# Rope queries of the latent heads made pair by pair, a second query buffer for every second head, and their zeros on GpSimd

## The chip, the cores and the metric

The kernel runs on one core of a Trainium2 chip. The metric is the device time of one execution in microseconds (us). Before the change three runs took 2487.42, 2492.72 and 2490.44 us: the median is 2490.44 us.

## The reference, cut to what matters

A trunk of two layers works on 256 latent tokens and 256 context tokens of width 2048, batch 1. The first layer runs two kinds of attention heads side by side and projects their gated outputs back to the stream; the second is a gated DeltaNet layer. The change lies in the first layer, in its eight latent-attention heads (MLA). The queries, keys and values of such a head come from low-rank latents; a query has 128 plain dimensions (`qn`) and 64 rotated ones (`qr`), and the rotated key part `kr` is common to all heads:

```
q = to_heads(rmsnorm(cq) @ w_qb, 8)            # 192 = 128 plain + 64 rope, per head
kv = to_heads(rmsnorm(ckv) @ w_kvb, 8)         # 256 = 128 key + 128 value
s_lat = (qn @ kn.T + rope(qr) @ rope(kr).T) * 192 ** -0.5      # latent keys
s_ctx = (qn @ kn_c.T + rope(qr) @ kr_c.T) * 192 ** -0.5        # context keys
p = softmax over both;  o = p_lat @ v + p_ctx @ v_c
```

The context tokens get the same attention over context keys alone. All inputs and outputs are float32.

## The kernel before, in words

**Tiling.** Activations lie with features on the 128 partitions and the 512 tokens (256 latent, 256 context) along the free axis. A matrix product with a weight tile of 128 by 128 is `dense`: each float32 factor is split in a rounded part and a remainder (`hi` and `lo`, or the two halves of `hx`, `cx`, `gx`), and three matmuls (lines L90, L91, L92) add hi·hi, hi·lo and lo·hi into a PSUM tile `mm`, of which there are two. A weight is loaded on the SyncE queue (`raw`, four buffers, L71), ScalarE casts it to `whi` (L77) and VectorE makes `wlo` (L78); both have three buffers.

**The stage around the change.** The layer runs seven neighbourhood heads, then makes the latents `craw` (eight tiles of 128 by 512), then loads the eighth neighbourhood head's inputs (`na7`). Now `cx`, which takes the place of `hx` in SBUF, receives in its first half `ch` the latents' hi parts (ScalarE, L468) and lo parts (VectorE, L469, `cx<-craw,cx`), and in its second half `qr` the rope queries. When `craw` has been read, its place is given to a pool with three buffers `mraw`, for the modulation weights of the second layer, and one of the size `lacc`. `attend` of the eighth neighbourhood head follows, then the rope queries of all eight latent heads, in four pairs: a `dense` of 12 matmuls from one weight of 2048 columns, zeros for the other head's 64 partitions (ScalarE, L481), and `roped`, which scales (L449), multiplies by a permutation on TensorE (`pp`, L451), combines with sine and cosine (L453 to L455), and writes hi and lo parts into `qr`. Then each of the eight heads makes `qT`, `kT` and `vT` (12 matmuls each) and runs `attend`: scores `sp` (L365), row maximum `mx` (VectorE, L389), exponential `pr` (ScalarE, L392), sum and scaling (L394, L395), transposes `pt` (L398), hi and lo parts `PT` (L357, L358), the product `po` with the values, and the gate (L405). `qT`, `kT` and `vT` have one buffer each.

**What sets the order.** In this layer the instructions aren't issued in the order of the source: a planner places them on each engine by its own estimate of when operands are ready, source order first among those that are. Each engine then works through its list strictly in that order. Between the heads lie steps of `ahead`, a generator that computes modulation chunks of the second layer: a chunk of 512 columns needs 16 TensorE matmuls into `pmod` (L141) from eight `mraw` loads of 512 KB (L136), then a copy and four transposes `pmt`. Each `mraw` load covers two of the 16 matmuls. Four chunks (2, 3, 8 and 9) fall in this stage. In the trace each float32 matmul (`pmod`, `pp`) shows as two.

After the heads, `gx` takes the place of `cx`: the gated outputs are split again (L502, L503) and the output projection begins; on VectorE four further chunks (L175, L177, `lacc`) run beside it.

Of the kernel before, what the change touches and what calls it, by code (L numbers as in the profile page):

```python
# [10 lines left out]
AF = mybir.ActivationFunctionType  # L11
ALU = mybir.AluOpType
# [6 lines left out]
T = 512  # L19
# [7 lines left out]
def trunk_kernel(ctx: ExitStack, tc: tile.TileContext, g):  # L27
    nc = tc.nc
    V, A, PE, P = nc.vector, nc.scalar, nc.tensor, nc.gpsimd
# [14 lines left out]
    def cst(name, shape, src=None):  # L44
        t = const.tile(shape, F32, name=name, tag=name)
        if src is not None:
            nc.scalar.dma_start(t, src)
        return t
# [3 lines left out]
    ones = cst("ones", [128, 128])  # L52
# [16 lines left out]
    def load_raw(src, n=1024):  # L69
        raw = wp.tile([128, 1024], F32, name="raw", tag="raw", bufs=4)  # L70
        nc.sync.dma_start(raw[:, :n], src)  # L71
        return raw
# [8 lines left out]
    def load_split(src, n=2048):  # L81
        return [split(load_raw(src[:, c:min(n, c + 1024)], min(1024, n - c)), min(1024, n - c))
                for c in range(0, n, 1024)]

    def dense(ps, w, off, kt, xh, xl, k0=0, sl=slice(0, T), first=True, last=True):
        for k in range(kt):
            c = off + k * 128
            wh, wl = w[c // 1024]
            c = slice(c % 1024, c % 1024 + 128)
            PE.matmul(ps, wh[:, c], xh[:, k0 + k, sl], start=first and k == 0, stop=False)  # L90
            PE.matmul(ps, wh[:, c], xl[:, k0 + k, sl], start=False, stop=False)  # L91
            end = PE.matmul(ps, wl[:, c], xh[:, k0 + k, sl], start=False, stop=last and k == kt - 1)  # L92
        return end.ins
# [166 lines left out]
    with tc.tile_pool(name="s0", bufs=2) as tp, tc.tile_pool(name="s0p", bufs=1, space=PSUM) as ps:  # L260
# [37 lines left out]
        for j, (k0, n) in enumerate(GROUPS):  # L298
            ahead = mods_of(j + 1) if j < end else iter(())
            for i in range(0, NS, 2):  # L300
                own = i < NP
                p = [pz[i + e] if own else mm_tile() for e in range(2)]
# [16 lines left out]
    with tc.tile_pool(name="ab", bufs=2, reuse_waits="tile") as tp, \  # L319
            tc.tile_pool(name="abp", bufs=2, space=PSUM, reuse_waits="tile") as ps:  # L320
        u, last_mm = NS, None
        mr = tc.alloc_tile_pool(name="mr", bufs=2)
# [21 lines left out]
        for j in range(NS, KT):  # L344
            p = unit(hh, hl)
# [3 lines left out]
        def parts(src, name, n=T, scale=1.0, pool=None, bufs=1):  # L349

            t = (pool or tp).tile([128, 2, n], F32R, name=name, tag=name, bufs=bufs)
            both(t[:, 0], t[:, 1], src, scale)
            return t
# [53 lines left out]
        def keep(p, name):  # L407
            t = tp.tile([128, T], F32, name=name, tag=name, bufs=1)
            A.copy(t, p)
            return t  # L410
# [33 lines left out]
        def roped(p, scale, parts_of):  # L444
            out = tp.tile([128, T], F32, name="rope", tag="rope", bufs=1)
            if scale == 1.0:
                A.copy(out, p)
            else:
                A.mul(out, p, scale)  # L449
            pp = ps.tile([128, S], F32, name="pp", tag="tr", bufs=TR)  # L450
            PE.matmul(pp, perm, out[:, :S], start=True, stop=True)  # L451
            t = tp.tile([128, S], F32, name="rtmp", tag="mtmp")
            V.tensor_tensor(t, pp, sinT, op=ALU.mult)  # L453
            V.tensor_tensor(out[:, :S], out[:, :S], cosT, op=ALU.mult)
            V.tensor_tensor(out[:, :S], out[:, :S], t, op=ALU.add)  # L455
            for r, hi, lo in parts_of:
                both(hi, lo, out[r])
# [5 lines left out]
        ch, qr = cx[:, 0], cx[:, 1]  # L463
        for i, gain in enumerate((q_gain, kv_gain)):
            for k in range(4):
                j = 4 * i + k
# [4 lines left out]
        mr = tc.alloc_tile_pool(name="mr2", bufs=2, reuse_waits="tile")  # L471
        ahead = later(mr, ((1, (2, 3, 8), 0),))

        rows = slice(0, 64), slice(64, 128)
        attend(*na7)
        w = load_split(g["ab_wqr"])
        for j in range(4):
            p = mm_tile()
            dense(p, w, j * 512, 4, ch, ch[:, 8:])
            for e in range(2):  # L480
                A.activation(qr[rows[1 - e], 4 * j + 2 * e:4 * j + 2 * e + 2],  # L481
                             ones[rows[1 - e], 0:1].unsqueeze(2).broadcast_to([64, 2, T]), AF.Copy, scale=0.0)
            roped(p, MLA_SCALE, [(rows[e], *[qr[rows[e], 4 * j + 2 * e + i] for i in range(2)]) for e in range(2)])
        for h in range(8):
            w = load_split(g["ab_wb"][h], 1536)
            o = []
            for j, (k0, name, sc) in enumerate(((0, "qT", MLA_SCALE), (4, "kT", 1.0), (4, "vT", 1.0))):
                p = mm_tile()
                last_mm = dense(p, w, j * 512, 4, ch, ch[:, 8:], k0)
                o.append(keep(p, name) if name == "vT" else parts(p, name, scale=sc))  # L490
            steps(ahead, 1)
            attend(*o, 8 + h, None, ([qr[:, 2 * h + i] for i in range(2)], [kr[:, i] for i in range(2)]))

# [12 lines left out]
        for j in range(KT):  # L506
# [3 lines left out]
            p = unit(gh, gl, g["ab_wo"][j])  # L510
# [129 lines left out]
    with tc.tile_pool(name="dn", bufs=2, reuse_waits="tile") as tp, \  # L640
# [12 lines left out]
        ch = cons[:, 0:768].rearrange("p (a n) -> p a n", a=6)  # L653
# [3 lines left out]
        p = dunit(U_BA, FULL)  # L657
# [562 lines left out]
        for st in range(-2, 64 + LAG):  # L1220
            i, n = st // 4, st % 4
            j, m = (st - LAG) // 4, (st - LAG) % 4
# [86 lines left out]
        for u in [v for e in range(KT - NE) for v in (e, NE + e)]:  # L1309
            k0 = 24 if u < NE else 0  # L1310
            w = load_split(g["dn_wo"][u][:, 128 * k0:], 4096 - 128 * k0)
            p = mm_tile() if i % 2 else ps.tile([128, T], F32, name="mm2", tag="ks")
            if i < KT - 1:
                dense2(p, w, 0, 32 - k0, gx, k0=k0)
            else:
                p = p[:, :S]
# [123 lines left out]
```

## Time and profile before

| | us |
|---|---|
| median of three runs | 2490.44 |
| profiled execution, its own time | 2493.04 |
| its span, from first to last instruction | 2491.2 |
| TensorE busy in the span | 2428.2 (97%) |
| VectorE busy | 1762.8 (71%) |
| ScalarE busy | 1105.6 (44%) |
| GpSimd busy | 161.1 (6%) |
| the stage, from `na7`'s first scores to the second output tile | about 687.6 to 907 |

The profiled execution is 2.6 us above the median, and 1.8 us of its time lie outside the span. Rows of the timeline give the start and the length in us, the engine, the line, the operation, the tiles written and read, and in brackets the idle time before and what ended it. A row of the chain of waits gives start, length and the piece of work. TensorE rows overlap, as matmuls are pipelined: the pitch from one to the next is what a matmul costs, and the busy time overstates it. The mean granted clock was 0.992.

### The profile page before, as it was taken

The numbers are of one execution on the slowest core, as the hardware profiler recorded it, in microseconds if no ns is written. First come the engines' busy times: TensorE is split into PE (matmuls) and PEld (weight loads), VectorE is DVE, ScalarE is ACT, GpSimd is POOL, SyncE is SP. The second block draws the span as 40 slices with busy tenths as digits, with TensorE's granted clock in tenths as the row PEclk, the third lists the DMA queues.
The fourth block names the chain that finished last, engine by engine and source line by source line (L and its number), as shares of the span: only waits on it lengthen the run. The fifth ranks groups of instructions, "written<-read, shape, count | busy, mean of one in ns | idle before, by whom it ended". The sixth has DMA issues, their size and how long they took to land.

```text
span 2491.2 us, 42483 instructions
## 1 busy us (share of the span) xinstructions
PE 2428.2 (97%) x16110; PEld 1963.1 (79%) x16110; DVE 1762.8 (71%) x3538; ACT 1105.6 (44%) x2446; POOL 161.1 (6%) x165
## 2 busy tenths in 40 slices
PE   6999999999989999999999999999999999999998
PEld 4557888888858878858998989987777777777787
DVE  4654678883356687856998988885777777777765
ACT  4223332333254432257565655634444544445453
POOL 0000000000000000020011101000000000012000
PEclk9999999999999999999999999999999999999999
DMA  8872645542253366664665666774343333336454
GB/s 252 282 277 87 200 154 172 169 157 84 88 187 110 102 198 204 226 210 136 195 173 158 179 178 180 204 201 108 87 116 103 115 112 98 106 100 184 148 193 141
DMA packets 254940, 397.24 MB, mean 159 GB/s; under 512 B 122257, under 2 KB 163857, under 8 KB 254609
## 3 DMA queue, kind: packets, MB, share of 16 engines
q1 hardware_dynamic: 253584, 393.00, 52.0%
q8 instruction: 127, 2.08, 0.3%
q10 hardware_dynamic: 1152, 1.54, 0.2%
q14 instruction: 77, 0.62, 0.1%
HBM read 356.94 MB, written 35.39 MB: 157 GB/s over the span
## 4 chain that ended last, share of the span: by engine, by line
PE 88%; issue 5%; DMA 3%; DVE 2%; ACT 1%; SPq 0%; POOL 0%; DVEq 0%; POOLq 0%; ACTq 0%
PE mm L90 21%; PE mm L91 20%; PE mm L92 20%; PE pks L1033 3%; PE pmod L141 3%; PE ptr L1045 2%; PE sp L365 2%; PE mm L105 2%; PE po L365 1%; DMA mraw<-dn_wm 1%; PE ptr L1078 1%; PE psu L1064 1%; PE pks L1064 1%; PE pt L398 1%; PE mm L107 1%
## 5 line engine op out<-in xcount | busy, mean ns | idle before, releaser
L90 PE MATMUL mm<-hx,whi 128*128 128x512 f32 (+1 forms) x2304 | 843.7, 366 | 2.3 <-ACT t L664 2.2
L91 PE MATMUL mm<-hx,whi 128*128 128x512 f32 (+1 forms) x2304 | 820.6, 356 | 2.5 <-issue 2.5
L92 PE MATMUL mm<-hx,wlo 128*128 128x512 f32 (+1 forms) x2304 | 819.4, 356 | 0.6 <-DVE wlo L78 0.6
L77 ACT CAST whi<-raw 128x1024 fp32r<-128x1024 f32 (+2 forms) x346 | 338.6, 980 | 701.4 <-PE mm L91 502.3
L78 DVE TENSOR_TENSOR wlo<-raw,whi 128x1024 fp32r<-128x1024 f32 (+2 forms) x346 | 394.3, 1142 | 204.3 <-ACT whi L77 198.2
L90 PEld LDWEIGHTS mm<-hx,whi 128*128 128x128 f32 x2304 | 438.8, 190 | 106.3 <-issue 27.0
L92 PEld LDWEIGHTS mm<-hx,wlo 128*128 128x128 f32 x2304 | 438.6, 190 | 65.1 <-issue 4.2
L91 PEld LDWEIGHTS mm<-hx,whi 128*128 128x128 f32 x2304 | 438.8, 190 | 61.4 <-issue 9.2
L177 DVE SCALAR_TENSOR_TENSOR lacc<-mraw,cond,lacc 128x512 f32<-128x512 f32 x300 | 208.6, 746 | 0.7 <-DMA mraw<-dn_wm 0.7
L585 DVE SCALAR_TENSOR_TENSOR acc<-cin,taps,acc 128x508 f32<-128x508 f32 (+3 forms) x256 | 187.2, 731 | 20.3 <-ACT acc L576 17.2
L105 PE MATMUL mm<-hx,whi 128*128 128x512 f32 x480 | 173.1, 404 | 0.1
L1055 DVE SCALAR_TENSOR_TENSOR vl<-ptr,egm,vh 128x128 fp32r<-128x128 f32 x224 | 64.7, 346 | 95.1 <-ACT rf L1052 37.9
L107 PE MATMUL mm<-hx,wlo 128*128 128x256 f32 x457 | 128.4, 281 | 1.3 <-DVE wlo L1139 1.2
L141 PE MATMUL pmod<-mraw,cond 128*32 128x512 f32 (+2 forms) x640 | 98.4, 508 | 28.1 <-DMA mraw<-ab_wm 18.8
L1139 DVE TENSOR_TENSOR wlo<-raw,whi 128x1024 fp32r<-128x1024 f32 x84 | 102.5, 1221 | 13.5 <-ACT whi L1131 13.4
L105 PEld LDWEIGHTS mm<-hx,whi 128*128 128x128 f32 x480 | 88.9, 188 | 24.5 <-issue 5.0
L816 DVE SCALAR_TENSOR_TENSOR outer<-L,bv,X 128x31 f32<-128x31 f32 (+15 forms) x248 | 99.4, 401 | 6.4 <-POOL X L811 0.5
L90 PE MATMUL mm<-gx,whi 128*128 128x512 f32 x256 | 100.3, 394 | 3.4 <-DVE x1B L515 2.4
L599 ACT ACTIVATE ac<-acc 128x128 f32<-128x128 f32 x160 | 37.4, 300 | 144.2 <-DVE acc L585 144.1
L91 PE MATMUL mm<-gx,whi 128*128 128x512 f32 x256 | 100.4, 392 | 0.5 <-DVE gx L503 0.5
L92 PE MATMUL mm<-gx,wlo 128*128 128x512 f32 x256 | 99.8, 391 | 0.0
L1049 ACT ACTIVATE vh<-ptr,egm 128x128 fp32r<-128x128 f32 x224 | 71.3, 374 | 57.1 <-PE ptr L1045 55.2
(301 smaller groups left out, 3648.5 us busy)
## 6 DMA issues: line engine op xcount, KB each, us to landing
raw<-dn_w SPq DMA_DIRECT2D x194, 512.0 KB
mraw<-dn_wm SPq DMA_DIRECT2D x96, 512.0 KB
mraw<-ab_wm SPq DMA_DIRECT2D x88, 512.0 KB
raw<-ab_w SPq DMA_DIRECT2D x66, 512.0 KB
raw<-dn_wo SPq DMA_DIRECT2D x64, 512.0 KB
raw<-ab_wo SPq DMA_DIRECT2D x32, 512.0 KB
raw<-ab_w SPq DMA_DIRECT2D x32, 256.0 KB
spt<-sp SPq DMA_DIRECT2D x64, 128.0 KB
```

The costliest lines, as they stand in the source:

```text
L77: A.copy(hi[:, :m], raw[:, :m])
L78: V.tensor_tensor(lo[:, :m], raw[:, :m], hi[:, :m].bitcast(F32), op=ALU.subtract)
L90: PE.matmul(ps, wh[:, c], xh[:, k0 + k, sl], start=first and k == 0, stop=False)
L91: PE.matmul(ps, wh[:, c], xl[:, k0 + k, sl], start=False, stop=False)
L92: end = PE.matmul(ps, wl[:, c], xh[:, k0 + k, sl], start=False, stop=last and k == kt - 1)
L105: PE.matmul(p2, wh[:, c], x[:, :, k0 + k], start=start, stop=stop)
L107: PE.matmul(p2[:, 0], wl[:, c], x[:, 0, k0 + k], start=False, stop=False)
L141: PE.matmul(pmod[32 * q:32 * q + 32, :m], cond[:, 4 * kg + q, :], raw[c // 1024][:, half + c % 1024:half + c % 1024 + m], start=kg == 0, s ...
L177: V.scalar_tensor_tensor(acc[:, s], raw[:, q], cond[:, k, s:s + 1], acc[:, s], op0=ALU.mult, op1=ALU.add)
L585: V.scalar_tensor_tensor(o3[:, :, i0:i1], p3[:, :, i0 + d:i1 + d], taps[:, ch, t:t + 1], o3[:, :, i0:i1], op0=ALU.mult, op1=ALU.add)
L816: V.scalar_tensor_tensor(o, L[:, rows, k:k + 1].broadcast_to([128, n, m]), bv[:, k:k + 1], X[:, k:k + 1, cols].broadcast_to([128, n, m]), ...
L1139: V.tensor_tensor(w, raws[j], h.bitcast(F32), op=ALU.subtract)
```

## The change

The rope queries of pair j are now made by a function `rope_pair(j)`, which loads only the 512 weight columns of its pair. Pair 0 is made before the first latent head; pairs 1, 2 and 3 are made in the heads 1, 3 and 5, between their `vT` and their `attend`. The plain queries of heads 1, 3, 5 and 7 go into the buffer `lacc` of the `mr2` pool instead of `qT`. The zeros are written by GpSimd as a constant minus itself, where ScalarE multiplied a constant by 0. Line numbers after the change are 7 higher from L498 on.

```diff
         attend(*na7)
-        w = load_split(g["ab_wqr"])
-        for j in range(4):
+
+        def rope_pair(j):
+            w = load_split(g["ab_wqr"][:, 512 * j:512 * j + 512], 512)
             p = mm_tile()
-            dense(p, w, j * 512, 4, ch, ch[:, 8:])
+            dense(p, w, 0, 4, ch, ch[:, 8:])
             for e in range(2):
-                A.activation(qr[rows[1 - e], 4 * j + 2 * e:4 * j + 2 * e + 2],
-                             ones[rows[1 - e], 0:1].unsqueeze(2).broadcast_to([64, 2, T]), AF.Copy, scale=0.0)
+                one = ones[rows[1 - e], 0:1].unsqueeze(2).broadcast_to([64, 2, T])
+                P.tensor_tensor(qr[rows[1 - e], 4 * j + 2 * e:4 * j + 2 * e + 2], one, one, op=ALU.subtract)
             roped(p, MLA_SCALE, [(rows[e], *[qr[rows[e], 4 * j + 2 * e + i] for i in range(2)]) for e in range(2)])
+
+
+        rope_pair(0)
         for h in range(8):
             w = load_split(g["ab_wb"][h], 1536)
             o = []
             for j, (k0, name, sc) in enumerate(((0, "qT", MLA_SCALE), (4, "kT", 1.0), (4, "vT", 1.0))):
                 p = mm_tile()
                 last_mm = dense(p, w, j * 512, 4, ch, ch[:, 8:], k0)
-                o.append(keep(p, name) if name == "vT" else parts(p, name, scale=sc))
+                o.append(keep(p, name) if name == "vT" else
+                         parts(p, "lacc", scale=sc, pool=mr) if name == "qT" and h % 2 else parts(p, name, scale=sc))
+            if h % 2 and h < 7:
+                rope_pair(h // 2 + 1)
             steps(ahead, 1)
             attend(*o, 8 + h, None, ([qr[:, 2 * h + i] for i in range(2)], [kr[:, i] for i in range(2)]))
```

The planner moves much within the stage; behind it, from early in the second layer on, the lists of all engines are the same as before. Three places matter for the prediction.

On GpSimd, from the first layer's modulation (`hx<-mh,hx`) to the start of the second layer, the list before was:

```order
L208 TENSOR_TENSOR rs<-ms,half 128x4
L243 TENSOR_TENSOR hx<-mh,hx 128x512 x11
L208 TENSOR_TENSOR rs<-ms,half 128x4 x3
L243 TENSOR_TENSOR hx<-mh,hx 128x512 x11
L798 MEMSET U 64x16x32
```

Now eight zeros (`cx<-ones`) stand between the latents' norms and the next one:

```order
L208 TENSOR_TENSOR rs<-ms,half 128x4
L243 TENSOR_TENSOR hx<-mh,hx 128x512 x11
L208 TENSOR_TENSOR rs<-ms,half 128x4 x2
L483 TENSOR_TENSOR cx<-ones 64x1024 x8
L208 TENSOR_TENSOR rs<-ms,half 128x4
L243 TENSOR_TENSOR hx<-mh,hx 128x512 x11
L805 MEMSET U 64x16x32
```

All eight zeros stand together, right behind the latents' norms: the first waits only for the place of `hx` to come free.

On VectorE, at the start of the stage (`sp<-sp,bias` is the bias on `na7`'s scores), the list before was:

```order
L387 TENSOR_TENSOR sp<-sp,bias 128x256
L78 TENSOR_TENSOR wlo<-raw,whi 128x1024
L389 TENSOR_REDUCE mx<-sp 128x1
L387 TENSOR_TENSOR sp<-sp,bias 128x256
L469 TENSOR_TENSOR cx<-craw,cx 128x512 x3
L389 TENSOR_REDUCE mx<-sp 128x1
L469 TENSOR_TENSOR cx<-craw,cx 128x512 x5
L358 TENSOR_TENSOR vt<-pv,vt 128x512
L394 RECIPROCAL rc<-sm 128x1
```

Now the lo parts stand closer together behind both biases:

```order
L78 TENSOR_TENSOR wlo<-raw,whi 128x512
L387 TENSOR_TENSOR sp<-sp,bias 128x256 x2
L469 TENSOR_TENSOR cx<-craw,cx 128x512
L389 TENSOR_REDUCE mx<-sp 128x1 x2
L469 TENSOR_TENSOR cx<-craw,cx 128x512 x7
L358 TENSOR_TENSOR vt<-pv,vt 128x512
L394 RECIPROCAL rc<-sm 128x1 x2
L389 TENSOR_REDUCE mx<-sp 128x1
L78 TENSOR_TENSOR wlo<-raw,whi 128x1024
```

The work is the same; one weight split is ahead of it, and both row maxima stand behind the first of the eight lo parts.

On TensorE, right behind the first 24 matmuls from `cx` (before: rope pairs 0 and 1; now: rope pair 0 and head 0's query), the list before was:

```order
L92 MATMUL mm<-cx,wlo 128x512
L141 MATMUL pmod<-mraw,cond 32x512 x4
L365 MATMUL sp<-kT,qT 128x256 x3
L398 MATMUL pt<-ident,pr 128x128 x4
L141 MATMUL pmod<-mraw,cond 32x512 x2
L365 MATMUL sp<-kT,qT 128x256 x3
```

and now the scores come directly behind the 24 matmuls, then head 0's key (12 matmuls, of which the last three are shown), and then:

```order
L90 MATMUL mm<-cx,whi 128x512
L91 MATMUL mm<-cx,whi 128x512
L92 MATMUL mm<-cx,wlo 128x512
L141 MATMUL pmod<-mraw,cond 32x512 x2
L398 MATMUL pt<-ident,pr 128x128 x8
L90 MATMUL mm<-cx,whi 128x512
```

The modulation matmuls come later and in smaller groups: over the four chunks the 64 matmuls stood in groups of 4, 2, 1, 2, 3, 2, 2, 4, 6, 4, 2 (chunks 2 and 3), 4, 4, 2, 6 (chunk 8) and 5, 1, 4, 2, 2, 2 (chunk 9); now they stand in groups of 2, 4, 1, 1, 4, 2, 2 (chunk 2), 1, 2, 3, 2, 1, 5, 2 (chunk 3), 2, 4, 2, 2, 6 (chunk 8) and 6, 2, 2, 6 (chunk 9).

## The prediction

> **What bounds the kernel now.** I read the page's busy shares and chain first, then a table of stretches, then the chain and the timeline of the stage.
>
> ```profile
> PE 2428.2 (97%) x16110; PEld 1963.1 (79%) x16110; DVE 1762.8 (71%) x3538; ACT 1105.6 (44%) x2446; POOL 161.1 (6%) x165
> PE 88%; issue 5%; DMA 3%; DVE 2%; ACT 1%; SPq 0%; POOL 0%; DVEq 0%; POOLq 0%; ACTq 0%
> 687.60:744.80 57.20, 49.83 (x220) 28.14 (x219) 31.67 (x61) 31.02 (x51) 0.00 (x0) 0.97 0.57 186
> 744.80:874.00 129.20, 129.20 (x740) 103.69 (x739) 78.30 (x172) 57.33 (x132) 0.00 (x0) 1.00 0.35 113
> 900.00:907.00 7.00, 3.13 (x14) 2.00 (x13) 5.45 (x11) 3.25 (x6) 0.00 (x0) 0.93 0.67 243
> ```
>
> TensorE bounds the kernel. The columns of a stretch are its length and the busy time of PE, PEld, DVE, ACT and POOL. From 744.8 to 874 TensorE is never idle, so a shorter path elsewhere buys nothing there; the change can only win or lose at the start of the stage (687.6 to 744.8) and at its end, where about 4 us are idle. The chain of waits shows what the start waits for and gives the prices of TensorE's pieces:
>
> ```profile
> 696.48 3.98 DMA mraw<-dn_wm
> 711.97 3.84 DMA mraw<-dn_wm
> ...
> 717.22 0.43 PE pp L451 x2
> ...
> 718.67 4.14 DMA mraw<-dn_wm
> 723.95 4.47 DMA mraw<-dn_wm
> ...
> 741.80 2.97 PE sp L365 x12
> 744.77 0.23 PE mm L90
> 749.95 0.44 PE pt L398 x4
> 750.39 0.94 PE sp L365 x8
> 758.26 1.32 PE po L365 x11
> 770.65 1.00 PE pmod L141 x8
> 772.23 0.98 PE pmod L141 x4
> 789.36 1.84 PE pmod L141 x12
> ```
>
> Per matmul: 0.23 us at 512 columns (0.25 for scores), 0.12 at 256, 0.11 for a transpose. A `pmod` group of two (x4 in the trace) takes 0.98 us and one of four (x8) takes 1.00: up to four run side by side, so the number of groups counts, and a group of six counts as two (1.84).
>
> TensorE's work in 687.6 to 744.8 before: 84 matmuls of `dense` 19.3, 18 wide scores 4.5, 6 narrow 0.7, 12 `pt` 1.3, 18 `po` 2.2, `pv` and `pmt` 0.9, four `pp` 1.7, 12 `pmod` groups 11.8; together 42.4 of 57.2 us. So 14.8 us are idle (more than the busy column admits, since that counts stretched matmuls). What can be won is below these 14.8 plus 4.
>
> **ScalarE's zeros, removed.** They stood on the path:
>
> ```profile
> L481 ACT ACTIVATE cx<-ones 64x1024 fp32r<-64x1024 f32 x8 | 8.4, 1054 | 0.1
> 693.32 6.39 ACT L481 ACTIVATE cx<-ones 64x1024 fp32r<-64x1024 f32 x6
> 692.72 0.68 DVE L389 TENSOR_REDUCE mx<-sp 128x1 f32<-128x512 f32 x1
> 701.28 0.69 ACT L392 ACTIVATE pr<-sp,mx 128x512 f32<-128x512 f32 x1
> ```
>
> Six of them kept the exponentials of `na7` until 701.28, although the second row maximum was ready at 693.4. With them gone the exponentials can run near 695. That alone is a gain of some 6 us on this chain.
>
> **GpSimd's zeros, added.** This form isn't in the trace. The nearest rows, grouped by shape:
>
> ```profile
> L820 POOL TENSOR_TENSOR X<-X,bv 128x1024 f32<-128x1024 f32 x7 | 14.4, 2051 | 95.2 <-DVE X L818 95.2
> L1185 POOL TENSOR_TENSOR hx<-re,hx 128x1024 fp32r<-128x1024 f32 x4 | 9.7, 2414 | 10.3 <-ACT hx L1184 10.3
> ```
>
> 2.05 us with a repeated operand, 2.41 with the rounded output; the zeros have both, and I take 2.2: 17.6 us of GpSimd in place of 8.4 of ScalarE. GpSimd is idle there, and head 0 needs only the first. The length itself costs nothing. But these rows show a second price:
>
> ```profile
> 1100.30 2.90 POOL L243 TENSOR_TENSOR hx<-mh,hx 128x512 fp32r<-128x512 f32 x2 [2.72 <-ACT mh L241]
> 1100.66 2.82 DVE L238 SCALAR_TENSOR_TENSOR hx<-mh,mod,hx 128x256 fp32r<-128x256 f32 x2
> L238 DVE SCALAR_TENSOR_TENSOR hx<-mh,mod,hx x20: 473/480/1522, 68.4 to 1102.0; 128x256 fp32r<-128x256 f32 x20
> 1092.99 1.31 POOL L243 TENSOR_TENSOR hx<-mh,hx 128x512 fp32r<-128x512 f32 x1 [0.41 <-ACT mh L241]
> 1093.30 0.48 DVE L235 SCALAR_TENSOR_TENSOR mh<-x1B,Am,rb 128x256 f32<-128x256 f32 x1
> 2240.74 2.83 POOL L1185 TENSOR_TENSOR hx<-gin,hx 128x1024 fp32r<-128x1024 f32 x1
> 2239.80 4.33 DVE L585 SCALAR_TENSOR_TENSOR acc<-cin,taps,acc 128x508 f32<-128x508 f32 x2
> L585 DVE SCALAR_TENSOR_TENSOR acc<-cin,taps,acc x256: 443/743/2751, 1124.7 to 2264.9; 128x510 f32<-128x510 f32 x48, 128x508 f32<-128x508 f32 x48, 128x255 f32<-128x255 f32 x16, 128x254 f32<-128x254 f32 x16
> ```
>
> L238 has two tensors from SBUF. Beside two GpSimd instructions, two of them took 2.82 us, where the median of one is 0.48: each waited for the GpSimd instruction before it. L235, whose second tensor is in PSUM, took its 0.48 us in the middle of one. Beside GpSimd's 1024 elements, two L585 took 4.33 against 0.74 each. The engines alternate: with one VectorE instruction let in, GpSimd's 2.4 became 2.83, so the pair has a period of the GpSimd time plus 0.4.
>
> The Trainium skill speaks against the change with the same rule: in "SBUF — State Buffer", section "Who interferes with whom", a VectorE instruction with two SBUF inputs contends with a GpSimd instruction that reads SBUF, and the one that starts later blocks until the other ends. The trace agrees (0.48 to about 1.4 us beside L243). By it the sum is the +6.4 below; without it, about -7.
>
> **What that hits.** The eight lo parts L469 read `craw` and `cx`, both in SBUF; they gate the first 36 matmuls, and after the last one the loads of `mraw` begin:
>
> ```profile
> 688.51 0.43 DVE L387 TENSOR_TENSOR sp<-sp,bias 128x256 f32<-128x256 f32 x1 [4.03 <-PE sp L365]
> 693.32 3.09 DVE L469 TENSOR_TENSOR cx<-craw,cx 128x512 fp32r<-128x512 f32 x5
> 696.48 7.60 SPq L136 DMA_DIRECT2D mraw<-dn_wm  x5
> 700.60 3.12 PE L141 MATMUL pmod<-mraw,cond 128*32 128x512 f32 x8 [3.65 <-DMA mraw<-dn_wm]
> ```
>
> Before, five took 3.09 us, and 0.07 us after the end of the last the first load was issued; it landed 4.1 us later. Now GpSimd's first zero starts when the last matmul that reads `hx` is done, near 688.1, at a period of 2.2 + 0.4 = 2.6. VectorE's list from there: a weight split (blocked by zero 1), two biases, lo 0 (blocked by zero 2), two maxima, lo 1 (zero 3) to lo 6 (zero 8, to 688.1 + 8 x 2.6 = 708.9), lo 7 (free, 709.5). Head 0's key needs lo 7, and ends at 710.2. `mraw` is issued at 709.6 and lands at 713.7, where TensorE has nothing else ahead in its list. Then a `pmod` group 1.0, `pt` 0.9, head 0's value 2.8, a `pmod` group 1.0: 719.4. The `pt` are ready by then: behind lo 7 VectorE needs some 4 us.
>
> By 719.4 TensorE has done 48 `dense` 11.0, 6 wide scores 1.5, 6 narrow 0.7, `pv` 0.4, 8 `pt` 0.9, two groups 2.0: 16.5 of 31.8 us. So 15.3 us are idle, as much as in the whole start before (14.8): **+0.5**.
>
> **Rope pairs spread, second buffer.** The waits of the four pairs are these (total, times, longest):
>
> ```profile
> ACT cx L357 <- DVE rope L455: 13.6, 4, 4.5
> ```
>
> From there TensorE's list has a `dense` of 12 or scores between any two short pieces, and the rope pairs 1 to 3 lie among heads where TensorE was always busy. Their waits, before one behind the other, are covered; without that cover each pair would cost up to a quarter of the 13.6 us, 3.4. The split of the weight in four costs no more elements. With `lacc` the next head's query can leave PSUM early. I cost these at nothing beyond the removal of the idle time counted above.
>
> **The `pmod` groups** number 12 + 5 + 7 = 24 before and 7 + 8 + 6 + 6 = 27 now (six as two): 3 x 0.98 = **+2.9**, from 0 (if they fall into waits) to 2.9.
>
> **New waits for `mraw`.** Chunk 9 now stands in groups of 6, 2, 2 and 6 at the end of the last heads. The six empty all three buffers; the next group needs a load of 4.1 us behind some 3 us of TensorE's work (`pv`, `po`, `pt`, scores), then the next buffer about 1.2 behind it, and so on: **+3**, from 0 to 6. The end of the stage keeps its 4 us.
>
> Sum against the profiled execution: 0.5 + 2.9 + 3.0 = +6.4, so 2499.4. That execution, 2493.04, lies 2.6 above the median of the runs, so for the median: **2496.8, rounded 2497**. Ends: zeros of 2.05 or 2.41 us change eight periods by -1.2 or +1.7; with the bounds of the other terms the sum runs from -0.7 to +11.1: 2490 to 2502.
>
> **The rivals.** A measurement of this kernel tells about 0.2% (5 us) from no change.
>
> *No contention, or harmless: faster.* If the zeros, whose operand is one repeated element, keep nobody waiting, lo 7 is done near 696.4 as before, `mraw` lands at 700.6, and the walk reaches its end at 706.2 instead of 719.4. The sum is 6.4 - 13.2 = -6.8: 2484. For it: no row shows a GpSimd instruction with only repeated operands. Against it: both rows of 1024 elements that overlap such VectorE work block it.
>
> *Contention, but the rest is hidden: same.* The groups and the new waits fall into idle time; only +0.5 to +3 remain: 2491 to 2493. For it: the planner put each group where it thought TensorE idle. Against it: after the start hardly any idle time is left.
>
> *More loss: slower.* The alternation is less kind to VectorE, or later zeros also hold up the scaling L395, so that the start ends 4 us later, and `mraw` loads starve more than chunk 9: +12, 2502. It decides as soon as a blocked lo part takes over 3 us.
>
> *The change doesn't do what it says*, as the pairs fall back to where they were: the list of TensorE rules it out.
>
> **How the numbers follow.** Contention with its costs (2497, own range 2490 to 2502) 50%, hidden rest 22%, no contention 20%, more loss 8%. The first gives slower in 8 of 10 cases and same otherwise; the second same in 8 of 10; the third faster in 7 of 10, else same; the fourth slower. Slower: 0.40 + 0.02 + 0.08 = 0.50; faster: 0.14 + 0.02 + 0.01 for a sum that is too high throughout = 0.17; same 0.33. The range that leaves out no more than two in ten reaches to the case without contention and to the loss: 2484 to 2504.
>
> **What would show it.** GpSimd's eight `cx<-ones` near 688 to 709, at 2.2 us and a period of 2.6; L469 at some 2.6 us for one instead of 0.68; the first `mraw` issue near 709.6; TensorE idle some 15 us before 720 and hardly after; more than 25 `pmod` groups. L469 near 0.68 beside the zeros would make it wrong, and so would a start that ends before 710.

## The result, and the profile after

The changed kernel takes 2507.88 us (median of four runs, 2505.18 to 2510.43), against 2490.57 for the kernel before on the same chip: a ratio of 1.0066, 95% interval 1.0053 to 1.0080. It is slower, as forecast, but by some 16 to 17 us where 6.4 were forecast, and the time lies above the range. The profiled execution took 2509.47 us, of which the span is 2507.7; its mean granted clock was 0.988, against 0.992 before.

The busy shares and the chain's shares on the page after look almost as before; TensorE still bounds the kernel, with the same number of instructions:

```profile
PE 2436.3 (97%) x16110; PEld 1966.6 (78%) x16110; DVE 1771.1 (71%) x3540; ACT 1102.5 (44%) x2444; POOL 176.2 (7%) x173
PE 88%; issue 5%; DVE 3%; DMA 2%; ACT 1%; SPq 0%; POOL 0%; DVEq 0%; POOLq 0%; ACTq 0%
```

The timeline of the start of the stage shows the zeros and what stands beside them (start, length, engine, line, tiles, count):

```profile
689.26 17.99 POOL L483 TENSOR_TENSOR cx<-ones 64x1024 fp32r<-64x1024 f32 x8 [37.57 <-PE mm L92]
689.58 2.12 DVE L78 TENSOR_TENSOR wlo<-raw,whi 128x512 fp32r<-128x512 f32 x1 [3.78 <-ACT whi L77]
692.29 1.71 DVE L469 TENSOR_TENSOR cx<-craw,cx 128x512 fp32r<-128x512 f32 x1
695.12 13.28 DVE L469 TENSOR_TENSOR cx<-craw,cx 128x512 fp32r<-128x512 f32 x7
...
708.47 1.28 SPq L136 DMA_DIRECT2D mraw<-dn_wm  x3
```

Seven lo parts take 13.28 us where five took 3.09 before, and the first `mraw` load of the stage is issued at 708.47 instead of 696.48. The chain of waits runs through them, and further on meets a load of chunk 9 and VectorE work at the end of the stage:

```profile
703.12 5.29 DVE cx L469 x3
708.47 4.10 DMA mraw<-dn_wm
712.71 1.92 PE pmod L141 x4
714.63 1.86 PE pt L398 x8
...
864.99 1.02 PE pmod L141 x8
866.02 7.26 DMA mraw<-dn_wm
873.32 1.92 PE pmod L141 x4
...
909.24 2.65 DVE lacc L177 x4
916.20 1.32 DVE lacc L177 x2
```

The `pmod` group of two and the eight transposes at 712.71 and 714.63 take 1.92 and 1.86 us, where the prediction's rows have 0.98 and some 0.9.

The table of TensorE's waits at the end of the stage (total, times, longest, in us) reads, before:

```profile
PE mm L90 <- DVE x1B L515: 2.4, 1, 2.4
PE mm L90 <- ACT gx L502: 1.0, 1, 1.0
PE mm L91 <- DVE gx L503: 0.5, 1, 0.5
```

and after:

```profile
PE mm L90 <- ACT gx L509: 2.2, 1, 2.2
PE po L365 <- DVE PT L358: 0.9, 1, 0.9
PE mm L90 <- DVE x1B L522: 0.8, 1, 0.8
PE po L365 <- ACT PT L357: 0.6, 1, 0.6
PE mm L91 <- DVE gx L510: 0.5, 1, 0.5
```

Where the time went can be read by taking the same TensorE instruction in both traces and subtracting its start. This offset (median over 25 us) is 1.3 us before the stage, where nothing was changed; 14.6 when the stage has ended; 20.7 at 1150, after the start of the second layer; 20.0 at 1290; 15.2 at 1325; 15.8 at the end. So the stage lost 13.3 us, the start of the second layer 6.1, and a piece of the second layer near 1310 gave 4.9 back.

That last piece is no gain of the change. Eleven of the fourteen kernels of the experiments show the same drop there, of 3.9 to 5.4 us, whichever part of the change they have. In the profile of the kernel before, TensorE stands still for 2.3 us at this place, for nothing that the profile shows, and has half its clock for 6.8 us behind it. The three kernels without the full drop show a stop of 2.2 us at the same place, the eleven one of 0 to 1.3, and the changed kernel 0.4. The rows of 1310 to 1320 show it, of the kernel before and then of b_lacc below, a kernel with the drop (columns as in the prediction's table; behind the five busy times stand the granted clock, the DMA's busy share and GB/s):

```profile
1310.00:1320.00 10.00, 7.66 (x72) 6.02 (x59) 6.00 (x13) 1.16 (x2) 1.04 (x2) 0.66 0.51 149
1310.00:1320.00 10.00, 10.00 (x176) 8.51 (x176) 9.48 (x21) 5.25 (x7) 0.89 (x2) 1.00 0.62 190
```

Why some executions stop there stayed open.

The clock matters in the stage, too. In these stretches TensorE was granted half its clock, first two of the kernel before, then three of the changed kernel:

```profile
701.20:704.60 3.40, 3.40 (x11) 1.15 (x9) 0.65 (x2) 3.38 (x8) 0.00 (x0) 0.50 0.73 246
906.00:909.40 3.40, 2.75 (x7) 2.23 (x8) 3.40 (x7) 1.59 (x4) 0.00 (x0) 0.50 0.63 208
706.20:716.20 10.00, 6.57 (x20) 3.35 (x18) 7.31 (x13) 1.59 (x4) 1.05 (x1) 0.50 0.57 193
873.30:876.70 3.40, 3.38 (x11) 1.28 (x13) 0.00 (x0) 0.38 (x1) 0.00 (x0) 0.50 0.48 190
917.70:924.40 6.70, 5.70 (x13) 4.07 (x14) 6.70 (x12) 3.42 (x6) 0.00 (x0) 0.50 0.71 209
```

What TensorE does there takes about twice as long (a matmul of 512 columns 0.43 us instead of 0.23), so half of its busy time in them is lost: 3.1 us before, 7.8 after. Outside its busy time TensorE idles 11.2 us in the stage before (675 to 950) and 19.0 after (676.3 to 964.6). So of the 13.3 us that the stage lost, 7.8 are more idle time and 4.7 are more time at half clock. All five stretches lie in or behind idle time of TensorE, but not every wait brings one: a_memz below waits 2.5 us until 859.4 without one. What decides it is not shown.

### The profile page after: what moved, and what is told of

Same layout as the page of the kernel before. It is cut to its first block, busy times and chain, and to the rows that moved or that the text cites. A ratio compares the mean times of both kernels' runs of the same rounds, so it can differ in the third digit from the quotient of the medians.

```text
span 2507.7 us, 42497 instructions
## 1 busy us (share of the span) xinstructions
PE 2436.3 (97%) x16110; PEld 1966.6 (78%) x16110; DVE 1771.1 (71%) x3540; ACT 1102.5 (44%) x2444; POOL 176.2 (7%) x173
## 4 chain that ended last, share of the span: by engine, by line
PE 88%; issue 5%; DVE 3%; DMA 2%; ACT 1%; SPq 0%; POOL 0%; DVEq 0%; POOLq 0%; ACTq 0%
PE mm L90 21%; PE mm L91 20%; PE mm L92 20%; PE pmod L141 3%; PE pks L1040 3%; PE ptr L1052 2%; PE sp L365 2%; PE mm L105 2%; PE po L365 1%; PE ptr L1085 1%; PE psu L1071 1%; PE pks L1071 1%; DMA mraw<-dn_wm 1%; PE pt L398 1%; PE mm L107 1%
## 5 line engine op out<-in xcount | busy, mean ns | idle before, releaser
L1146 DVE TENSOR_TENSOR wlo<-raw,whi 128x1024 fp32r<-128x1024 f32 x84 | 102.5, 1221 | 13.4 <-ACT whi L1138 13.3
L309 DVE TENSOR_TENSOR zs<-zs,mm 128x512 f32<-128x512 f32 x72 | 49.2, 687 | 68.7 <-PE mm L92 68.5
```

Of the source, the lines that this page charges most:

```text
L1146: V.tensor_tensor(w, raws[j], h.bitcast(F32), op=ALU.subtract)
```

## The experiments

The theory behind the forecast: GpSimd's zeros read SBUF and block VectorE's lo parts; that holds back the release of `craw`, and so the `mraw` loads. Its rivals: the zeros are harmless and the spread pairs or the second buffer cost the time; or the planner's new lists do. The change has three parts (spread pairs, second buffer, zeros on GpSimd), so most kernels undo one or do one alone. Since the planner makes new lists for nearly every edit, pairs of kernels with the same lists count most. Differences in us are (ratio - 1) x 2491.

### a_memz: the zeros by memset

```diff
-                P.tensor_tensor(qr[rows[1 - e], ...], one, one, op=ALU.subtract)
+                P.memset(qr[rows[1 - e], ...].bitcast(F32), 0.0)
```

> The changed kernel with one operation replaced: the eight zeros on GpSimd are a memset, which reads nothing, in place of a constant minus itself; the lists of all engines are otherwise the same. Theory (the subtraction's SBUF reads block VectorE's lo parts of the latents, which holds the release of their place and the first modulation load for 12 us): L469 falls from 1.9 to 0.62-0.68 us each, the first mraw load of the stage is issued near 697 instead of 708.5, the walk's end (first matmul of head 1's query) comes 11 to 13 us earlier, and the time is 2495 (2491 to 2499). Rival A (any GpSimd instruction on the same tiles blocks, by its own length; a memset of 1024 elements took 0.96 us): L469 near 1.1 us, the first mraw near 700, 2500 to 2502. Rival B (the zeros do not set the end; the whole loss is the spread pairs and the second buffer): 2505 to 2510.

Measured: 2494.46 us, ratio 1.0012 (1.0004 to 1.0020), 13.4 us below the changed kernel. Its timeline at the same place:

```profile
689.27 7.97 POOL L482 MEMSET cx<- 64x1024 f32 x8 [37.55 <-PE mm L92]
690.89 0.68 DVE L469 TENSOR_TENSOR cx<-craw,cx 128x512 fp32r<-128x512 f32 x1
692.68 4.29 DVE L469 TENSOR_TENSOR cx<-craw,cx 128x512 fp32r<-128x512 f32 x7
697.05 1.28 SPq L136 DMA_DIRECT2D mraw<-dn_wm  x3
```

GpSimd writes the same tiles at the same time, and each lo part takes its 0.68 us. So writing these tiles blocks nothing, which leaves the reading: rivals A and B fall. The Trainium skill states it so ("SBUF — State Buffer", section "Who interferes with whom": a VectorE instruction with two SBUF inputs contends with a GpSimd instruction that reads SBUF, not with one that only writes it); the trace agrees, with 0.68 beside the memset and 1.93 beside the subtraction.

### b_poolz and b_memz: the zeros alone, in the kernel before

```diff
-                A.activation(qr[rows[1 - e], ...], ones[...], AF.Copy, scale=0.0)
+                P.tensor_tensor(qr[rows[1 - e], ...], one, one, op=ALU.subtract)    # b_poolz
+                P.memset(qr[rows[1 - e], ...].bitcast(F32), 0.0)                    # b_memz
```

> The kernel before with the zeros alone moved to GpSimd (constant minus itself). Theory: the lo parts take 1.9 us each, the first mraw load is issued near 708 instead of 696.5; the exponentials of na7 come 6 us earlier but the walk to the first heads ends no earlier, so 2490 to 2497 (0 to +6). Rival A (zeros harmless, the move frees ScalarE): 2484 to 2486. Rival B (the planner's new lists of the second layer decide): lists there hardly differ in this kernel, so no change of 6 us and more behind 1066.

> The kernel before with the zeros alone moved to GpSimd, as a memset; its lists are those of the kernel with the subtraction in the same place. Theory: no reads, no blocking: L469 0.62-0.68 us each, first mraw near 696, exponentials of na7 6 us earlier than before, 2480 to 2488, that is 6 to 13 below the same kernel with the subtraction. Rival (blocking by any GpSimd access): L469 near 1.1 us, 2487 to 2492. Rival (zeros do not matter): equal to the kernel before within 2 us.

Measured: with the subtraction 2499.77 us, ratio 1.0024 (1.0011 to 1.0037), +6.0, at the upper edge of what was expected; with the memset 2483.68 us, ratio 0.9972 (0.9960 to 0.9984), -7.0. The lists of the two are the same, so the 13.0 between them is the blocking alone, with what it brings behind it. The groups of the subtraction's kernel (busy us, mean ns of one):

```profile
L482 POOL TENSOR_TENSOR cx<-ones 64x1024 fp32r<-64x1024 f32 x8 | 18.0, 2249 | 38.1 <-PE mm L92 37.6
L469 DVE TENSOR_TENSOR cx<-craw,cx 128x512 fp32r<-128x512 f32 x8 | 15.3, 1972 | 0.0
```

Freeing ScalarE of the zeros is worth 7 us here, with the new lists that come with it; writing them on GpSimd as a subtraction instead of a memset takes 13 away.

### a_half: the zeros in pieces of half the length

```diff
-                P.tensor_tensor(qr[..., 4 * j + 2 * e:4 * j + 2 * e + 2], one, one, op=ALU.subtract)
+                for i in range(2):
+                    P.tensor_tensor(qr[..., 4 * j + 2 * e + i], one, one, op=ALU.subtract)
```

> The changed kernel with each zero instruction cut in two of half the length (16 of 512 columns instead of 8 of 1024; the same elements). The planner makes new lists, so the start of the stage is what counts. Theory (a blocked VectorE instruction waits for the one GpSimd instruction in flight, and one is let in between any two): GpSimd near 1.1 us each, L469 near 1.1 to 1.2 us instead of 1.93, the last lo part and the first mraw load near 702 to 703 instead of 708.5, so some 6 us earlier. Rival A (VectorE waits until GpSimd's share of the port is used up, whatever the pieces): L469 on average 1.9 us, first mraw at 708. Rival B (what blocks is starting a GpSimd instruction): twice the starts, first mraw later than 708.5.

Measured: 2505.55 us, ratio 1.0052 (1.0036 to 1.0069). The groups of this kernel:

```profile
L484 POOL TENSOR_TENSOR cx<-ones 64x512 fp32r<-64x512 f32 x16 | 21.4, 1356 | 38.1 <-PE mm L92 37.6
L469 DVE TENSOR_TENSOR cx<-craw,cx 128x512 fp32r<-128x512 f32 x8 | 10.9, 1415 | 0.0
```

The first `mraw` load is issued at 703.15, 5.3 us earlier than in the changed kernel: a lo part waits for one GpSimd instruction, and a shorter one blocks for less. Each piece is longer than half of 2.18, and the lo part longer than the 1.1 to 1.2 expected, because one VectorE instruction is let in between any two. The time itself (-3.5 us against the changed kernel, intervals that overlap) says little, and the lists differ.

### a_dep: the same subtractions, but behind the lo parts

```diff
-                one = ones[rows[1 - e], 0:1].unsqueeze(2).broadcast_to([64, 2, T])
+                one = ch[rows[1 - e], 15, 0:1].bitcast(F32).unsqueeze(2).broadcast_to([64, 2, T])
```

> The changed kernel with the same eight subtractions on GpSimd and the same lists on all engines, but the repeated operand is an element of the last lo part of the latents instead of a constant, so that the first zero waits until VectorE has written all eight lo parts. Theory (the loss of 13 us is not the subtraction as such but that it runs beside the lo parts): L469 0.62-0.68 us, first mraw near 697, zeros from 697 to some 715, where they can block three weight splits and the rope combinations of pair 0: 2496 to 2500, most of the memset's gain. Rival A (the zeros only move the blocked time, since VectorE has two-input work all along): 2503 to 2508. Rival B (no loss left at all): 2493 to 2495.

Measured: 2499.40 us, ratio 1.0031 (1.0020 to 1.0042), 8.7 below the changed kernel and 4.7 above the memset. The groups between 687 and 722 us:

```profile
L483 POOL TENSOR_TENSOR cx<-cx 64x1024 fp32r<-64x1024 f32 x8 | 17.0, 2122 | 46.0 <-DVE cx L469 45.4
L469 DVE TENSOR_TENSOR cx<-craw,cx 128x512 fp32r<-128x512 f32 x8 | 5.0, 684 | 0.0
L395 DVE TENSOR_SCALAR pr<-pr,rc 128x512 f32<-128x512 f32 x2 | 4.1, 2110 | 0.0
L398 PE MATMUL pt<-ident,pr 128*128 128x128 f32 x12 | 2.0, 279 | 1.4 <-DVE pr L395 1.4
```

The lo parts are free again and the first `mraw` load is issued at 695.6. The zeros, as long as before, now block others: two weight splits and the scaling L395 of `na7` (2.11 us for one instead of 0.48), for which TensorE's transposes `pt` waited 1.4 us. So it is the place of the subtractions that costs, and two thirds of the loss go away with the order alone.

### a_nolacc and a_memz_nolacc: without the second buffer

```diff
-                         parts(p, "lacc", scale=sc, pool=mr) if name == "qT" and h % 2 else parts(p, name, scale=sc))
+                         parts(p, name, scale=sc))
```

> The changed kernel without the second query buffer: all heads use qT. The planner makes new lists. Theory (the buffer is worth little either way): 2505 to 2511. Rival A (head 7's query sits in the buffer lacc until its scores are done, so that the vector-engine chunks behind the heads, which need lacc, begin late and the end of the stage idles 7.7 instead of 4.6 us): 2502 to 2505, with the idle time of the end back near 4.6. Rival B (the buffer lets queries leave PSUM early and is worth a wait per second head): 2512 to 2518.

> The changed kernel with both suspects taken out: zeros by memset, and no second query buffer (its lists are those of the kernel without the buffer). What is left of the change are the spread pairs and ScalarE freed of the zeros. Theory (the two losses are separate and add: 13.4 for the blocked lo parts, 6.1 for what the buffer does to the lists): 2494.5 - 6.1 = 2488.4 (2486 to 2491), first mraw near 697, idle time at the end of the stage near 4. Rival A (they share one cause, or one hides the other): 2493 to 2496. Rival B (the spread itself costs nothing): 2484, as the kernel before with a memset.

Measured: 2501.75 us, ratio 1.0037 (1.0025 to 1.0049), with the subtraction; 2487.88 us, ratio 0.9989 (0.9978 to 1.0000), with the memset, as its theory expected. The blocking is worth 12.0 here (same lists). Without the buffer the time is 5.7 to 7.2 us lower (with the memset and with the subtraction): more than I expected, in the direction of rival A. But rival A's reason fails: the first `lacc` instruction of the chunks behind the heads (L175) starts at 887.5 with the buffer, as the first output matmul does, and at 889.2 without, 3.7 us after that matmul; nothing waits there for `lacc`. What differs is the list: without the buffer, chunk 9 stands in groups of 5, 1, 4, 2, 2 and 2 instead of 6, 2, 2 and 6.

### b_lacc and a_actz_nolacc: the buffer alone, the spread alone

> The kernel before with the second query buffer alone: the plain queries of heads 1, 3, 5 and 7 in lacc; pairs and zeros as before. Theory (with the buffer the planner lays chunk 9's groups closer together than its loads come, and packs VectorE's list behind the last head, whatever the pairs do): pmod waits for loads near 850 to 880 and 6 to 8 us idle at the end of the stage, 2494 to 2498. Rival A (the loss needs the spread pairs too): 2490 to 2492. Rival B (the buffer saves waits): 2485 to 2489.

> The kernel before with the spread pairs alone: pair 0 ahead, pairs 1 to 3 in heads 1, 3 and 5; zeros on ScalarE as before, one query buffer. Theory (the spread costs some 4.6 us, which is what it costs beside the memset if the parts add: 2488.4 against 2483.7, from more pmod groups and their loads): 2494 to 2497. Rival A (the spread is the gain that the change was to have, as pairs 1 to 3 no longer stand in the ramp): 2484 to 2488. Rival B (no difference): 2490 to 2492.

```diff
-                o.append(keep(p, name) if name == "vT" else parts(p, name, scale=sc))                       # b_lacc
+                o.append(keep(p, name) if name == "vT" else
+                         parts(p, "lacc", scale=sc, pool=mr) if name == "qT" and h % 2 else parts(p, name, scale=sc))
-        w = load_split(g["ab_wqr"])                                                                         # a_actz_nolacc
-        for j in range(4):
+        def rope_pair(j):
+            w = load_split(g["ab_wqr"][:, 512 * j:512 * j + 512], 512)
...
+            if h % 2 and h < 7:
+                rope_pair(h // 2 + 1)
```

Measured: the buffer alone 2489.26 us, ratio 0.9988 (0.9979 to 0.9997); the spread alone 2489.77 us, ratio 0.9988 (0.9979 to 0.9996). By the median each gains about 3 us, so my theory was wrong in both: neither part costs anything by itself. The spread has 26 `pmod` groups instead of 24 and is still not slower.

### a_actz: the change with its zeros left on ScalarE

```diff
-                P.tensor_tensor(qr[rows[1 - e], ...], one, one, op=ALU.subtract)
+                A.activation(qr[rows[1 - e], ...], ones[...], AF.Copy, scale=0.0)
```

> The changed kernel with the zeros back on ScalarE: spread pairs and second buffer, with new lists in which chunk 9 stands in groups of 4, 2, 2, 2 and 4. Theory (without blocked lo parts, and with chunk 9 laid looser than 6, 2, 2 and 6, nothing much is lost): first mraw near 696, 2489 to 2494. Rival A (spread and buffer together cost 9 us, whatever the zeros do: 2494.5 with the memset against 2485 to 2488 without the buffer): 2495 to 2498. Rival B (ScalarE's zeros hold the exponentials as before on top of that): 2500 to 2504.

Measured: 2486.84 us, ratio 0.9985 (0.9974 to 0.9996), so 3.7 us faster than the kernel before, and below all three ranges that I gave. All that makes the change slower comes with its third part: the blocking, and the other lists that the planner makes when GpSimd has the zeros.

### b_memz_lacc: the two gains together

```diff
-                A.activation(qr[rows[1 - e], ...], ones[...], AF.Copy, scale=0.0)
+                P.memset(qr[rows[1 - e], ...].bitcast(F32), 0.0)
...
-                o.append(keep(p, name) if name == "vT" else parts(p, name, scale=sc))
+                         parts(p, "lacc", scale=sc, pool=mr) if name == "qT" and h % 2 else parts(p, name, scale=sc))
```

> The kernel before with memset zeros on GpSimd and the second buffer, without spread pairs: the two parts that gained by themselves. Theory (they add; chunk 9 stands in groups of 6, 2, 2, 2 and 4, as with the buffer alone): 2483.7 - 3 = 2481 (2478 to 2485). Rival (the buffer's gain was covered by the ramp that the memset shortens): 2483 to 2487. Rival (head 7's layout costs as in the changed kernel): 2488 to 2491.

Measured: 2491.41 us, ratio 0.9998 (0.9986 to 1.0010): the gains of 7.0 and 3.0 don't add, they vanish. The third alternative came closest, though not by its reason: chunk 9 stands as with the buffer alone. From 1050 to 1150 us the offset grows by 3.1, where it shrank by 1.0 with the memset alone. This led to SyncE's list at the start of the second layer, which comes in two forms. In the changed kernel's timeline:

```profile
1082.70 0.33 SPq L71 DMA_DIRECT2D raw<-dn_w  x1
1085.00 30.89 SPq L136 DMA_DIRECT2D mraw<-dn_wm  x12
1115.95 0.42 SPq L71 DMA_DIRECT2D raw<-dn_w  x1
...
1128.31 0.33 SPq L547 DMA_DIRECT2D taps<-taps  x1
```

and in that of the kernel before:

```profile
1068.12 0.49 SPq L71 DMA_DIRECT2D raw<-dn_w  x1
1070.81 27.37 SPq L136 DMA_DIRECT2D mraw<-dn_wm  x11
1098.70 0.33 SPq L71 DMA_DIRECT2D raw<-dn_w  x1
```

Twelve loads of `mraw` in a row instead of eleven, and the weight (L71) behind them is issued 33.2 us after the one ahead of them instead of 30.6. TensorE then waits there, first after the change, then before it:

```profile
PE mm L90 <- ACT t L671: 4.0, 1, 4.0
```

```profile
PE mm L90 <- ACT t L664: 2.2, 1, 2.2
```

### a_memz_lacc3 and a_lacc3: the buffer undone at head 7 alone

```diff
-   parts(p, "lacc", scale=sc, pool=mr) if name == "qT" and h % 2 else
+   parts(p, "lacc", scale=sc, pool=mr) if name == "qT" and h % 2 and h < 7 else
```

> The changed kernel with the zeros by memset, and the second query buffer for heads 1, 3 and 5 alone; head 7's plain query goes to qT. Up to head 7 TensorE's list is that of the kernel with the memset; behind it chunk 9 now stands in groups of 5, 3, 2, 2 and 2 (and two more behind the first output matmul) instead of 6, 2, 2 and 6. Theory (the buffer costs its 6 us at head 7, through chunk 9's groups and the list behind them): no wait of over 1.5 us for chunk 9, 4 us idle at the end of the stage, 2487 to 2490. Rival A (the cost of the buffer lies in heads 1 to 5): 2493 to 2495. Rival B (half and half): 2490 to 2493.

> The changed kernel with one thing undone: head 7's plain query goes to qT instead of the second buffer; zeros stay subtractions on GpSimd. SyncE's list at the start of the second layer is again the one of the kernel before (eleven mraw loads in a row, then a weight, a mraw, a weight, a mraw, the taps), where the changed kernel has twelve, and chunk 9 stands in groups of 5, 3, 2, 2 and 2. Theory (contention costs its 13 us whatever the lists; chunk 9's groups and the order of these loads cost the other 7 to 9): 2484.2 + 13 = 2497 (2495 to 2500); offset against the kernel before unchanged within 1.5 us between 1050 and 1150. Rival (the contention is worth less once the end of the stage is loose): 2490 to 2494. Rival (head 7's buffer matters only beside the memset): 2504 to 2508.

Measured: 2484.17 us, ratio 0.9977 (0.9964 to 0.9989), with the memset: 8.7 below the same kernel with the buffer at all four heads and 3 below what I expected. With the subtraction 2495.68 us, ratio 1.0032 (1.0018 to 1.0047): 8.5 below the changed kernel, as expected, but the offset between 1050 and 1150 didn't stay within 1.5 us: it shrank by 3.4. The two differ by 13.7 (same lists). Up to head 7 TensorE's list is the changed kernel's. Behind it chunk 9 stands in groups of 5, 3, 2, 2, 2 and 2, SyncE's list has eleven loads, and TensorE's waits at the end of the stage are again those of the kernel before, shorter by 0.7 (a_memz_lacc3):

```profile
PE mm L90 <- DVE x1B L521: 1.7, 1, 1.7
PE mm L90 <- ACT gx L508: 1.0, 1, 1.0
PE mm L91 <- DVE gx L509: 0.5, 1, 0.5
```

### a_memz_p2: the buffer kept, the list changed

```diff
-            steps(ahead, 1)
+            steps(ahead, 2)
```

> The changed kernel with memset zeros, the second buffer kept for all four heads, and two steps of ahead in place of one between the heads, which lays the modulation groups otherwise: chunk 9 in groups of 6, 2, 2, 2 and 4, and SyncE's list at the start of the second layer with eleven mraw loads in a row. Theory (the list costs, not the buffer): 2484 to 2489, with the offset between 1050 and 1150 growing by less than 1.5 us. Rival (the buffer at head 7 costs by itself): 2492 to 2496 as with one step.

Measured: 2486.97 us, ratio 0.9987 (0.9974 to 1.0000): 6.2 below a_memz, which has the same parts with one step. The buffer is at head 7, chunk 9 stands in groups of 6, 2, 2, 2 and 4, no load of it is on the chain of waits, TensorE's waits at the end of the stage add up to 3.2 us (3.9 in the kernel before), and SyncE's list has eleven loads. (The offset between 1050 and 1150 grew by 1.9, a little over the 1.5 expected.) So the lists cost these 6 to 9 us, not the buffer.

### All kernels in one table

Pairs, buffer and zeros say which parts of the change a kernel has. "stage" is the growth of the offset against the kernel before from the start of the stage (675) to its end (950), "start of layer 2" from 1050 to 1150; both are from one profiled execution each.

| kernel | pairs spread | second buffer | zeros | `mraw` in a row | ratio | us | stage | start of layer 2 |
|---|---|---|---|---|---|---|---|---|
| changed | yes | 1, 3, 5, 7 | subtract | 12 | 1.0066 | +16.4 | +13.3 | +6.1 |
| a_half | yes | 1, 3, 5, 7 | subtract, halves | 12 | 1.0052 | +13.0 | +7.8 | +3.1 |
| a_nolacc | yes | no | subtract | 12 | 1.0037 | +9.2 | +5.2 | +1.5 |
| a_lacc3 | yes | 1, 3, 5 | subtract | 11 | 1.0032 | +8.0 | +8.1 | -3.4 |
| a_dep | yes | 1, 3, 5, 7 | subtract, later | 12 | 1.0031 | +7.7 | -0.2 | +6.3 |
| b_poolz | no | no | subtract | 11 | 1.0024 | +6.0 | +5.6 | +0.8 |
| a_memz | yes | 1, 3, 5, 7 | memset | 12 | 1.0012 | +3.0 | -2.4 | +4.2 |
| b_memz_lacc | no | 1, 3, 5, 7 | memset | 12 | 0.9998 | -0.5 | -1.8 | +3.1 |
| a_memz_nolacc | yes | no | memset | 12 | 0.9989 | -2.7 | -8.7 | +3.4 |
| b_lacc | no | 1, 3, 5, 7 | ScalarE | 11 | 0.9988 | -3.0 | +2.3 | -0.9 |
| a_actz_nolacc | yes | no | ScalarE | 11 | 0.9988 | -3.0 | -2.2 | +0.3 |
| a_memz_p2 | yes | 1, 3, 5, 7 | memset | 11 | 0.9987 | -3.2 | -7.3 | +1.9 |
| a_actz | yes | 1, 3, 5, 7 | ScalarE | 11 | 0.9985 | -3.7 | -5.1 | +0.2 |
| a_memz_lacc3 | yes | 1, 3, 5 | memset | 11 | 0.9977 | -5.7 | -5.8 | -1.8 |
| b_memz | no | no | memset | 11 | 0.9972 | -7.0 | -5.2 | -1.0 |

The start of the second layer costs +1.5 to +6.3 (mean 4.0) in the seven kernels with twelve loads, and -3.4 to +1.9 (mean -0.5) in the eight with eleven. I didn't change that order alone, so it is the likely cause and not a shown one. In the changed kernel most of the 6.1 us is again half clock: four stretches of 20.4 us in all, against three of 10.2 before, cost 4.0 us more by the same reckoning. So part of what this column shows is the clock of one execution.

Best are b_memz, one statement away from the kernel before, and a_memz_lacc3: both beat both kernels.

## Why the prediction was right in its direction and wrong in its size

**Right: the contention.** The rival without contention was 13.2 us below the forecast. Four pairs with the same lists measured 13.4, 13.0, 12.0 and 13.7. The first `mraw` load was forecast for 709.6 and issued at 708.47; the walk's end was forecast for 719.4, and head 1's query starts at 720.19. From 688.9 (where the walk starts, 1.3 us later by the offset) these are 31.3 us, 14.8 more than the 16.5 of work, where 15.3 were forecast. The price that was off is the period: a zero takes 1.89 us alone and 2.22 with a lo part let in, so the period is 2.30, not 2.6; the late start of the zeros (689.3 for 688.1) made up for half of that.

**Partly luck: how well the walk fits.** It costs waits as idle time and everything behind them at full clock. The group and the transposes behind the first load ran at half clock, 1.6 us longer than costed, and the load came 1.1 us early. In the pair of the changed kernel and a_memz, the group starts 11.4 us later with the subtraction (712.71 against 701.28) and head 1's query 13.2 later (720.19 against 707.02): the forecast 13.2 is right in its sum, but 1.7 of the measured 13.2 arise behind the load, nearly all at half clock, which the prediction left out. Its own rows had it: the granted clock of 0.97 in the first stretch, and the `pmod` group of four that took 3.12 us at 700.60 instead of 1.00.

**Right: the groups.** 27 groups of `pmod` were forecast and 27 are in the trace. But the spread alone, with 26, was no slower than the kernel before, so it isn't shown that their 2.9 us cost anything.

**Wrong in size: "New waits for `mraw`", +3.** The mechanism is as forecast: the group of six empties the buffers and the next group waits, on the chain for 7.26 us of a load (866.02). TensorE idles 4.2 us between 860 and 912, against none in the same stretch before (848 to 900), and the half clock behind the wait (873.30) costs 1.7 more: some 6, the upper bound that the text gave.

**Wrong: "The end of the stage keeps its 4 us."** TensorE's waits there add up to 5.0 us by the table above, against 3.9 before, and the half clock behind them lasts 6.7 us instead of 3.4, which costs 1.5 more. On VectorE four `lacc` instructions stand ahead of the last gates and `gx` parts (909.24, 2.65 us, on the chain), where VectorE had stood idle for 0.94 us before the last gate. I read the list up to the heads and took the end as unchanged.

**Wrong: nothing was taken for the start of the second layer.** The text ahead of the prediction says that the lists are the same from early in the second layer on, and the sum ended there; the stretch ahead of it, with the twelve loads, went uncounted: 6.1 us in the profiled execution.

**The last three go together,** and runs show what they are worth: undoing the buffer at head 7 (a_lacc3) gives 8.5 of the 16.4 us back, without touching the contention; with the same parts and another pacing (a_memz_p2) 6.2 come back. So the sum of the change, by runs, is -5.7 for what is left with a memset and the buffer at three heads, +8.7 for the lists that come with the buffer at head 7, and +13.4 for the blocking: +16.4. The sentence that failed is "With `lacc` the next head's query can leave PSUM early. I cost these at nothing": the buffer itself costs nothing (-3.0 alone), but with it the planner laid the groups of chunk 9, and what stands behind them, otherwise. What each of the three places is worth by itself is read from one profile each, not from runs.

**The case without contention** was put at 2484, faster. With the memset the changed kernel took 2494.5: the contention went, as that case said, but the list's 8.7 stayed. 2484 is what came when both were undone (a_memz_lacc3).

**Not explained:** 1.3 us before the stage, where the lists are equal, and the stop near 1310 in some executions. They make single executions differ by some 5 us from what the change does, and are why the differences here come from several runs each.

## What to carry to other kernels

A constant that GpSimd writes should be a memset, not arithmetic on a tile that it must read: here the same zeros at the same time cost 13 us more in one form than in the other, because VectorE's work with two SBUF inputs stood on the critical path. Before moving work to an idle engine, look at what the other engine does in those microseconds, and from which memory. Where a planner lays the work, an edit costs what its new lists cost, too: compare them to the end of the program, and cost each place where loads have changed their order. Cost a wait not by its idle time alone: look in the trace for the clock that was granted behind it.

## What was not expected of the hardware

The scaling L395 has a single tensor operand from SBUF (and a scalar for each partition), yet beside GpSimd's reads it took 2.11 us instead of 0.48 (a_dep), and 1.26 beside the pieces of half the length (a_half). The forecast took only work with two SBUF tensors for exposed; its rival of more loss named L395, without a price. The Trainium skill names this too ("SBUF — State Buffer", section "Who interferes with whom": `tensor_scalar` can enter a mode with two ports, when its operands allow it, and can then contend), and the trace agrees that it contends; which mode it ran in no run shows. The row maximum L389, which reads PSUM, took its 0.68 us throughout.

The sharing isn't even: a lo part of 0.68 us was stretched to 2.38, but the zero that let it in only from 1.89 to 2.22.
